# Differential attention: softmax difference, row sums and output squares moved off GpSimd and ScalarE onto VectorE

## The chip, the cores and the metric

The kernel runs on one core of one Trainium2 chip. The core has five engines with a queue each: TensorE (PE in the profile, with its weight loads as PEld), VectorE (DVE), ScalarE (ACT), GpSimd (POOL) and SyncE (SP), which here only issues DMAs. Each engine takes its instructions in the order in which they stand in its queue, and an instruction that waits holds up those behind it. The metric is the device time of one execution in microseconds (us).

## The reference

A two-layer encoder trunk for 1024 tokens of 1024 features, in float32. Layer 0 mixes tokens by differential attention, layer 1 by a state-space scan; each is followed by an MLP. The change touches layer 0's attention alone, cut here to its core:

```python
def block(q_blk):
    scores = jnp.einsum('bqhcd,bkhcd->bhcqk', q_blk, k, preferred_element_type=jnp.float32)
    p = jax.nn.softmax(scores, axis=-1)
    attn = (p[:, :, 0] - lam * p[:, :, 1]).astype(v.dtype)
    return jnp.einsum('bhqk,bkhe->bqhe', attn, v)

o = lax.map(block, qb)
o = o.transpose(1, 0, 2, 3, 4).reshape(b, s, N_HEADS, V_HEAD_DIM)
o = rms_norm(o, subln_gain) * (1.0 - lam_init)
return o.reshape(b, s, D_MODEL) @ w_o
```

There are 8 heads; each has two score maps (c = 0, 1) of 1024 x 1024, whose softmaxes are subtracted with the factor lambda before the product with the values. A head's output, 128 features per token, is then normalised by its root mean square.

## The kernel before

The program runs through the norm of x, the projections q, k and v, the attention, the output projection, the first MLP (beside which the state-space layer's matrices are prepared), the state-space layer with its gate, and the second MLP. Nearly all of it is bound to large matmuls.

The attention is cut into 64 tiles: 8 heads (h) times 8 blocks of 128 queries (qt). One tile passes through these steps, each a function of the kernel:

- `scores` (L395 to 407): for each of the two maps m, four matmuls of 512 columns into one `pss` of two banks: two against `kh`, the keys' high parts, and then two against `kl`, their low parts. There are two `pss`, so the scores of a tile's map wait until the exponentials of the same map in the tile before have read theirs.
- `maxima` (L409): one VectorE reduction of 128 x 1024 for each map.
- `exps` (L416): one ScalarE exponential for each map into `e0`, `e1`, with the row sums `s` written beside it.
- `combine` (L426): the factor `al` from the two row sums (a reciprocal and one more VectorE operation of one column), then `pd` = e0 + al * e1. It is done in two parts. Of the last 704 columns VectorE forms al * e1 (L434) and GpSimd adds e0 (L435); the first 320 columns VectorE does in one operation (L436). Then VectorE squares the row sum s0 into a column of `s2h` (L437).
- `transposes` (L440): eight transposes of `pd` on TensorE into two banks `pT`; `evacuate` (L450): ScalarE copies them to `pt`; `values` (L456): eight products with V into `po`. In the trace each of these eight float32 products is two records.
- `keep` (L462): ScalarE copies `po` to `osb` (L466), and then squares it with a sum into `ssh` (L467).

Once per head, `norm_o` adds `s2h` and `ssh`, takes the inverse root and scales `osb` (L476), and `turn_o` transposes it into `oT`, which ScalarE and VectorE (L485) split into high and low parts. `load_ops` (L382) loads a map's `q` (512 KB), `kh` and `kl` (two pieces of 256 KB each) from DRAM over SP's queue. There are three slots for each of the three, so the loads for a new head's second map wait until the scores of the first map of the last tile of the head before have been read from theirs.

The loops write the steps in a staggered order (`CF["order"]`), but a scheduler decides the order of the instructions in each engine's queue from its own estimates: another set of instructions can bring another order everywhere in the attention.

Of the kernel before, what the change touches and what calls it, by code (L numbers as in the profile page):

```python
# [10 lines left out]
F32 = mybir.dt.float32  # L11
# [6 lines left out]
P = 128  # L18
# [20 lines left out]
class WStream:  # L39
    """Weight tiles in the order of their use: loaded and split `ahead` tiles before that."""  # L40
# [50 lines left out]
def _build(ctx, tc, nc, a, out):  # L91
# [24 lines left out]
    # weights in the order of use  # L116
# [39 lines left out]
    # quarters of the columns by how much of their sums is done ahead: k 0 and 1, k 0 to 3, nothing  # L156
# [19 lines left out]
    def mm3(ps, w, n0, xs, nk=KT, halves=None):  # L176
        """ps [128, 1024] = W[:, n0:n0+128]^T X, in three passes that carry float32."""
# [13 lines left out]
    def mmh(ps, w, n0, xs, ks, t, start, stop):  # L191
        """The same for the k of one half and the tokens of one half."""
        c = slice(t * 512, t * 512 + 512)
        last = len(ks) - 1
        for kk, k in enumerate(ks):
            for i, (wt, x) in enumerate(((w[0], xs[0]), (w[0], xs[1]), (w[1], xs[0]))):
                nc.tensor.matmul(  # L197
                    ps, wt[:, kk, n0 : n0 + P], x[k][:, c], start=start and kk == 0 and i == 0, stop=stop and kk == last and i == 2
                )

    # ---------------------------------------------------------------- norm of x, transposed
# [5 lines left out]
    with tc.tile_pool(name="p0", bufs=8) as p0, tc.tile_pool(name="ps0", bufs=4, space=PSUM) as ps0:  # L207
# [46 lines left out]
        # lambda, on every partition  # L254
# [14 lines left out]
    # ---------------------------------------------------------------- q, k, v  # L269
# [100 lines left out]
    # ---------------------------------------------------------------- attention  # L370
# [7 lines left out]
    with tc.tile_pool(name="pb", bufs=2) as pb, tc.tile_pool(name="psb", bufs=2, space=PSUM) as psb:  # L378
# [13 lines left out]
        def scores(h, qt):  # L392
            if qt == 0:
# [3 lines left out]
                    small.tile([P, KT], F32, name="s2h", tag="s2h"),  # L397
# [18 lines left out]
        def exps(h, qt):  # L416
            w = work[h, qt]
            for m in range(2):
                e = pb.tile([P, S], F32, name=f"e{m}", tag=f"e{m}", bufs=CF["e"])
                s = small.tile([P, 1], F32, name="s", tag="s", bufs=6)  # L420
# [4 lines left out]
        def combine(h, qt):  # L425
            w = work[h, qt]  # L426
            s2h = heads[h][2]
            es, sums = w["e"], w["s"]
            al = small.tile([P, 1], F32, name="al", tag="al", bufs=4)
            nc.vector.reciprocal(al, sums[1])  # L430
            nc.vector.scalar_tensor_tensor(al, al, nlam, sums[0], op0=ALU.mult, op1=ALU.mult)
            pd = pb.tile([P, S], F32, name="pd", tag="pd", bufs=CF["pd"])
            n = CF["sp"]
            nc.vector.tensor_scalar(pd[:, n:], es[1][:, n:], al, None, op0=ALU.mult)  # L434
            nc.gpsimd.tensor_tensor(pd[:, n:], pd[:, n:], es[0][:, n:], op=ALU.add)  # L435
            nc.vector.scalar_tensor_tensor(pd[:, :n], es[1][:, :n], al, es[0][:, :n], op0=ALU.mult, op1=ALU.add)  # L436
            nc.vector.scalar_tensor_tensor(s2h[:, qt : qt + 1], sums[0], EPS * P, sums[0], op0=ALU.mult, op1=ALU.mult)  # L437
# [24 lines left out]
        def keep(h, qt):  # L462
            osb, ssh, s2h = heads[h]
# [3 lines left out]
            nc.scalar.activation(junk, osb[:, qt, :], AF.Square, accum_out=ssh[:, qt : qt + 1])  # L467

        def norm_o(h):
            osb, ssh, s2h = heads[h]  # L470
            # 1 / sqrt(mean o^2 + eps s0^2)
            rn = small.tile([P, KT], F32, name="rn", tag="rn")
            nc.vector.tensor_tensor(rn, s2h, ssh, op=ALU.add)
            nc.scalar.activation(rn, rn, AF.Ln, scale=1.0 / P)
# [17 lines left out]
        with tc.manual_schedule() if CF["man"] else ExitStack():  # L492
            stage = dict(S=scores, E=evacuate, K=keep, C=combine, M=maxima, X=exps, V=values, T=transposes)
            for i in range(n + 9):
# [8 lines left out]
                # a head's output, spread over the next tiles  # L503
# [11 lines left out]
    # ---------------------------------------------------------------- output projection, residual  # L515
# [7 lines left out]
    def acc_tile(name):  # L523
        """Two banks, as a tile or as two."""
# [7 lines left out]
    def pieces(ps):  # L532
        """(columns, bank or banks) of an accumulator."""
# [7 lines left out]
    class Norm:  # L541
        """The mean square of h over its features, as they come."""
# [26 lines left out]
        def per_token(self, rtok):  # L569
            """1 / root mean square as [c, j], token 8 c + j."""  # L570
# [52 lines left out]
    # ---------------------------------------------------------------- MLP  # L623
# [73 lines left out]
    # ---------------------------------------------------------------- S5 and GLU  # L697
# [83 lines left out]
class Prep:  # L781
    """The state-space layer's matrices, from its parameters alone, into DRAM.

    Rows of the state are (direction, p). Per group of channels:
    IN  [(j,h), (direction, re|im, p)]   a^(7-j) Bbar forward, a^j Bbar backward
    Y   [(direction, p), (re|im, j, h)]  Re and -Im of C a^(j+1) forward, C a^(8-j) backward
    K   [h', lag + 7, h]                 the kernel within a chunk of 8 tokens, with the skip
    R   [(direction, p), (cos|sin, n)]   of the angle of a^8 times n
    """
# [12 lines left out]
    def start(self, ps_pool, pool):  # L802
# [10 lines left out]
        # parameters as [(direction, p), g]  # L813
# [37 lines left out]
        # angles: theta, and 8 theta 2^k  # L851
# [22 lines left out]
        # (a - 1) / lambda  # L874
# [14 lines left out]
        # powers: a^l forward, a^(7-l) backward  # L889
# [16 lines left out]
        # mask of the diagonal blocks and of the diagonal  # L906
        self.mask = kp("mask", (P, 8))
        nc.gpsimd.memset(self.mask, 1.0)
        # keep where 0 <= p - 16 g <= 15
        nc.gpsimd.affine_select(self.mask, self.mask, [[-16, 8]], ALU.is_ge, 0.0, base=0, channel_multiplier=1)  # L910
        nc.gpsimd.affine_select(self.mask, self.mask, [[16, 8]], ALU.is_ge, 0.0, base=15, channel_multiplier=-1)
        # [p, h] = (p mod 16 == h)
# [7 lines left out]
        # skip times the norm's gain, by feature  # L920
# [6 lines left out]
    def tile(self, kt):  # L927
# [8 lines left out]
        def cmul(o, x, y, op, tmp, E=nc.gpsimd):  # L936
            """o = x[0] x[1] op y[0] y[1]"""
# [4 lines left out]
        # B, with the norm's gain  # L942
# [15 lines left out]
        # C and C a  # L958
# [17 lines left out]
        # the kernel at lag 0, both directions, and the skip  # L976
# [16 lines left out]
        # B by direction, zero in the other's rows  # L993
# [8 lines left out]
        for hf in range(4):  # L1002
# [8 lines left out]
            # IN, transposed  # L1011
# [14 lines left out]
            # Y  # L1026
# [4 lines left out]
            # the kernel at lags 1..8, [(lag, h), h']  # L1031
# [11 lines left out]
            # the rotation  # L1043
# [218 lines left out]
```

## Time and profile before

| | us |
|---|---|
| median of 3 runs | 2617.03 |
| lowest and highest run | 2615.14 and 2620.7 |
| span of the profiled execution | 2618.1 |
| of it, from the first scores to the first matmul of the output projection | 368.4 |

The profile is of one execution. The page gives each engine's busy time over the span, and the chain of work that ended last. A view by stretches gives each engine's busy time between two moments, with the granted clock of TensorE (1.00 is 2.4 GHz). A view of groups gives the mean length of equal instructions. A view in order of time gives the start of each instruction, its length and, in square brackets, how long its engine stood idle ahead of it and what ended that. Lengths of following instructions overlap a little, since engines are pipelined; what one costs in a full queue is read from start to start.

### The profile page before, as it was taken

The page shows a single profiled execution, that of the slowest core. Times are in us where ns is not written, and L with a number is a line of the kernel's source. Part 1 is how long each engine was busy: PE and PEld are TensorE (multiplying, and loading weights), DVE is VectorE, ACT ScalarE, POOL GpSimd, SP SyncE. Part 2 cuts the span into 40 slices and gives each one's busy share as a digit, 9 for nine tenths or more (in the row PEclk, how much of TensorE's full clock was granted, in tenths as well). Part 3 has the DMA queues.
Part 4 walks back from the last instruction along what each step waited for, and adds up shares of the span by engine and source line. Part 5 has one row for each costly group of instructions (what it writes and reads, how often), then busy time and mean ns, then how long its engine had stood idle before and what let it go on. Part 6 is the DMA issues. An engine that isn't in the chain of part 4 may idle for free.

```text
span 2618.1 us, 33770 instructions
## 1 busy us (share of the span) xinstructions
PE 2496.8 (95%) x12530; PEld 2071.0 (79%) x12530; DVE 1621.5 (62%) x3441; ACT 981.9 (38%) x1801; POOL 391.7 (15%) x452
## 2 busy tenths in 40 slices
PE   7999988888999999999999997899999999999998
PEld 6889877777777778788788876787888888888887
DVE  5664299999558987987973457994533333333332
ACT  5654276666433122122122137882331122112212
POOL 1211033333101431332341230000000000000000
PEclk9999999999999999999999998999999999999999
DMA  5768124131211222322332236553211111111112
GB/s 155 191 171 203 55 50 97 49 87 35 76 47 52 90 86 81 90 86 82 93 93 57 77 131 185 164 145 98 65 47 49 49 49 49 49 49 49 49 49 65
DMA packets 264964, 225.22 MB, mean 86 GB/s; under 512 B 41696, under 2 KB 248160, under 8 KB 264800
## 3 DMA queue, kind: packets, MB, share of 16 engines
q1 hardware_dynamic: 258912, 214.44, 28.8%
q10 hardware_dynamic: 5888, 8.63, 1.3%
q8 instruction: 99, 1.62, 0.3%
q14 instruction: 65, 0.53, 0.1%
HBM read 163.31 MB, written 51.31 MB: 82 GB/s over the span
## 4 chain that ended last, share of the span: by engine, by line
PE 61%; DVE 26%; ACT 4%; DMA 4%; issue 3%; SPq 1%; POOL 0%; DVEq 0%; ACTq 0%; POOLq 0%
PE psd L183 19%; PE psu L183 19%; PE psq L183 7%; DVE s2h L437 3%; DVE mx L413 3%; PE psw L183 3%; PE psh L197 3%; DVE tr L939 3%; DVE Rt L940 2%; ACT e L421 2%; DVE Rt L938 2%; DMA Rd<-Rt 2%; PE psg L183 2%; DVE wlo L67 2%; DVE pd L434 1%
## 5 line engine op out<-in xcount | busy, mean ns | idle before, releaser
L66 ACT ACTIVATE whi<-wraw 128x1024 fp32r<-128x1024 f32 (+1 forms) x177 | 186.8, 1055 | 971.1 <-PE psu L183 445.7
L658 DVE TENSOR_TENSOR hT<-hT,psd 128x1024 f32<-128x1024 f32 (+1 forms) x153 | 158.6, 1042 | 282.1 <-PE psd L183 282.1
L183 PE MATMUL psd<-sh,wlo 128*128 128x512 f32 x1024 | 332.3, 400 | 0.0
L183 PE MATMUL psd<-sh,whi 128*128 128x512 f32 x1024 | 328.0, 399 | 1.7 <-ACT ob L612 1.7
L183 PE MATMUL psd<-sl,whi 128*128 128x512 f32 x1024 | 326.7, 398 | 0.0
L183 PE MATMUL psu<-ah_u,whi 128*128 128x512 f32 x1024 | 318.7, 392 | 0.0
L183 PE MATMUL psu<-ah_u,wlo 128*128 128x512 f32 x1024 | 316.9, 391 | 0.0
L183 PE MATMUL psu<-al_u,whi 128*128 128x512 f32 x1024 | 316.8, 391 | 0.0
L67 DVE TENSOR_TENSOR wlo<-wraw,whi 128x1024 fp32r<-128x1024 f32 (+1 forms) x177 | 219.2, 1239 | 95.5 <-ACT whi L66 95.2
L640 DVE SCALAR_TENSOR_TENSOR mz<-psu,nacc 128x512 f32<-128x512 f32 x128 | 82.9, 685 | 281.5 <-PE psu L183 272.5
L183 PEld LDWEIGHTS psd<-sl,whi 128*128 128x128 f32 x1024 | 190.9, 188 | 44.4
L183 PEld LDWEIGHTS psd<-sh,whi 128*128 128x128 f32 x1024 | 190.0, 188 | 45.5 <-ACT ob L612 3.1
L183 PEld LDWEIGHTS psd<-sh,wlo 128*128 128x128 f32 x1024 | 191.1, 188 | 43.5
L183 PEld LDWEIGHTS psu<-ah_u,whi 128*128 128x128 f32 x1024 | 192.0, 188 | 42.1 <-issue 1.7
L183 PEld LDWEIGHTS psu<-al_u,whi 128*128 128x128 f32 x1024 | 192.4, 188 | 39.9
L183 PEld LDWEIGHTS psu<-ah_u,wlo 128*128 128x128 f32 x1024 | 192.1, 188 | 39.9
L421 ACT ACTIVATE e<-pss,mx 128x1024 f32<-128x1024 f32 x128 | 142.7, 1115 | 117.0 <-DVE mx L413 116.1
L435 POOL TENSOR_TENSOR pd<-pd,e 128x704 f32<-128x704 f32 x64 | 117.9, 1842 | 342.2 <-DVE pd L434 131.0
L413 DVE TENSOR_REDUCE mx<-pss 128x1 f32<-128x1024 f32 x128 | 150.8, 1210 | 2.4 <-PE pss L406 2.3
L460 PE MATMUL po<-V,pt 128*128 128x128 f32 x1024 | 136.1, 276 | 0.7 <-ACT pt L454 0.7
L460 PEld LDWEIGHTS po<-V,pt 128*128 128x128 f32 x1024 | 130.5, 193 | 6.8 <-ACT pt L454 1.1
L406 PE MATMUL pss<-kh,q 128*128 128x512 f32 x256 | 92.8, 444 | 42.0 <-ACT e L421 37.5
(311 smaller groups left out, 4361.3 us busy)
## 6 DMA issues: line engine op xcount, KB each, us to landing
wraw<-in_ffn_w_up_dram SPq DMA_DIRECT2D x64, 512.0 KB, 4.0
wraw<-in_ffn_w_down_dram SPq DMA_DIRECT2D x64, 512.0 KB, 3.5
wraw<-in_attn_w_qkv_dram SPq DMA_DIRECT2D x24, 512.0 KB, 6.1
xt<-in_x_dram SPq DMA_DIRECT2D x16, 512.0 KB, 6.4
zs<-z ACTq DMA_DIRECT2D x64, 128.0 KB, 5.2
q<-qs SPq DMA_DIRECT2D x16, 512.0 KB, 6.6
kh<-ks SPq DMA_DIRECT2D x32, 256.0 KB, 6.9
kl<-ks SPq DMA_DIRECT2D x32, 256.0 KB, 7.7
```

The costliest lines, as they stand in the source:

```text
L66: self.nc.scalar.activation(hi, t, AF.Copy)
L67: self.nc.vector.tensor_tensor(lo, t, f32(hi), op=ALU.subtract)
L183: nc.tensor.matmul(ps[t] if isinstance(ps, list) else ps[:, c], wt[:, k, n0 : n0 + P], x[k][:, c], start=k == 0 and i == 0, stop=k == nk - ...
L197: nc.tensor.matmul(ps, wt[:, kk, n0 : n0 + P], x[k][:, c], start=start and kk == 0 and i == 0, stop=stop and kk == last and i == 2)
L406: nc.tensor.matmul(ps[:, c], q[:, qt * P : (qt + 1) * P], k[:, c], start=i == 0, stop=i == 1)
L413: nc.vector.tensor_reduce(mx, w["ps"][m], axis=AX.X, op=ALU.min)
L421: nc.scalar.activation(e, w["ps"][m], AF.Exp, bias=w["mx"][m], scale=-1.0, accum_out=s)
L435: nc.gpsimd.tensor_tensor(pd[:, n:], pd[:, n:], es[0][:, n:], op=ALU.add)
L437: nc.vector.scalar_tensor_tensor(s2h[:, qt : qt + 1], sums[0], EPS * P, sums[0], op0=ALU.mult, op1=ALU.mult)
L460: nc.tensor.matmul(w["po"], w["pt"][:, k, :], V[:, k, h * P : (h + 1) * P], start=k == 0, stop=k == KT - 1)
L640: nc.vector.scalar_tensor_tensor(z, bank(ps, t), 0.0, rbc[:, c], op0=ALU.max, op1=ALU.mult)
L658: nc.vector.tensor_tensor(hT[:, m, c], hT[:, m, c], p, op=ALU.add)
```

## The change

In `combine` the three operations that form `pd` become one VectorE operation over all 1024 columns (L433 of the new kernel), and GpSimd has no part in the attention any more. The 64 squares of a row sum (L437) go: the exponentials now write their row sums into columns of a tile `sums` that is kept for a head, and `norm_o` squares them once per head (L471). In `keep` the square and sum of `osb` move from ScalarE to VectorE, in one operation that multiplies `po`, still in PSUM, by `osb` and writes the sum beside it (L463). `al` is formed by another form of operation of one column (L431). The factor 1/P moves from one place of the norm to another. The rest of the diff strips comments.

```diff
-                    small.tile([P, KT], F32, name="s2h", tag="s2h"),
+                    small.tile([P, 2, KT], F32, name="sums", tag="sums"),
...
-                s = small.tile([P, 1], F32, name="s", tag="s", bufs=6)
+                s = heads[h][2][:, m, qt : qt + 1]
                 nc.scalar.activation(e, w["ps"][m], AF.Exp, bias=w["mx"][m], scale=-1.0, accum_out=s)
...
             nc.vector.reciprocal(al, sums[1])
-            nc.vector.scalar_tensor_tensor(al, al, nlam, sums[0], op0=ALU.mult, op1=ALU.mult)
+            nc.vector.tensor_scalar(al, al, nlam, sums[0], op0=ALU.mult, op1=ALU.mult)
             pd = pb.tile([P, S], F32, name="pd", tag="pd", bufs=CF["pd"])
-            n = CF["sp"]
-            nc.vector.tensor_scalar(pd[:, n:], es[1][:, n:], al, None, op0=ALU.mult)
-            nc.gpsimd.tensor_tensor(pd[:, n:], pd[:, n:], es[0][:, n:], op=ALU.add)
-            nc.vector.scalar_tensor_tensor(pd[:, :n], es[1][:, :n], al, es[0][:, :n], op0=ALU.mult, op1=ALU.add)
-            nc.vector.scalar_tensor_tensor(s2h[:, qt : qt + 1], sums[0], EPS * P, sums[0], op0=ALU.mult, op1=ALU.mult)
+            nc.vector.scalar_tensor_tensor(pd, es[1], al, es[0], op0=ALU.mult, op1=ALU.add)
...
             nc.scalar.activation(osb[:, qt, :], w["po"], AF.Copy)
-            nc.scalar.activation(junk, osb[:, qt, :], AF.Square, accum_out=ssh[:, qt : qt + 1])
+            nc.vector.scalar_tensor_tensor(
+                junk, w["po"], 1.0 / P, osb[:, qt, :], op0=ALU.mult, op1=ALU.mult, accum_out=ssh[:, qt : qt + 1]
+            )
...
+            s2 = small.tile([P, KT], F32, name="s2", tag="s2")
+            nc.vector.scalar_tensor_tensor(s2, sums[:, 0, :], EPS, sums[:, 0, :], op0=ALU.mult, op1=ALU.mult)
             rn = small.tile([P, KT], F32, name="rn", tag="rn")
-            nc.vector.tensor_tensor(rn, s2h, ssh, op=ALU.add)
-            nc.scalar.activation(rn, rn, AF.Ln, scale=1.0 / P)
+            nc.vector.tensor_tensor(rn, s2, ssh, op=ALU.add)
+            nc.scalar.activation(rn, rn, AF.Ln)
```

The scheduler gives the attention another order on TensorE, VectorE and ScalarE; from the output projection on, the order is the one of before. Two places matter below.

VectorE in the middle of a head, before: one tile from one pair of maxima (`mx`, one for each map) to the next.

```order
L413 TENSOR_REDUCE mx<-pss 128x1 x2
L430 RECIPROCAL al<-s 128x1
L431 SCALAR_TENSOR_TENSOR al<-al,nlam,s 128x1
L434 TENSOR_SCALAR pd<-e_3620,al 128x704
L436 SCALAR_TENSOR_TENSOR pd<-e_3620,al,e_3617 128x320
L437 SCALAR_TENSOR_TENSOR s2h<-s 128x1
L413 TENSOR_REDUCE mx<-pss 128x1 x2
```

VectorE in the middle of a head, in the changed kernel:

```order
L430 RECIPROCAL al<-sums 128x1
L431 TENSOR_SCALAR al<-al,nlam,sums 128x1
L433 SCALAR_TENSOR_TENSOR pd<-e_3546,al,e_3544 128x1024
L413 TENSOR_REDUCE mx<-pss 128x1
L463 SCALAR_TENSOR_TENSOR junkb,ssh<-po,osb 128x128
L413 TENSOR_REDUCE mx<-pss 128x1
L430 RECIPROCAL al<-sums 128x1
```

The square of the row sum no longer stands ahead of the maxima, and the new sum of squares (of a tile two or more back) stands between the two maxima, so that one of them is behind a wait for ScalarE's copy of `po`.

TensorE at the start of the third head (tile 16), before: from the scores of its first map (the first two rows) to those of its second (the last two).

```order
L406 MATMUL pss<-kh,q 128x512 x2
L406 MATMUL pss<-kl,q 128x512 x2
L460 MATMUL po<-V,pt 128x128 x4
L447 MATMUL pT<-ident,pd 128x128 x2
L460 MATMUL po<-V,pt 128x128 x4
L447 MATMUL pT<-ident,pd 128x128 x6
L406 MATMUL pss<-kh,q 128x512 x2
L406 MATMUL pss<-kl,q 128x512 x2
```

TensorE at the same place in the changed kernel:

```order
L406 MATMUL pss<-kh,q 128x512 x2
L406 MATMUL pss<-kl,q 128x512 x2
L443 MATMUL pT<-ident,pd 128x128 x8
L406 MATMUL pss<-kh,q 128x512 x2
L406 MATMUL pss<-kl,q 128x512 x2
L456 MATMUL po<-V,pt 128x128 x8
```

The products with V have moved behind the scores of the second map, so these stand closer to those of the first. At other heads' starts four of the eight products stay ahead of them.

## Rows read from the trace of the kernel before

**Rows 1.** The page: busy time of each engine; shares of the chain that ended last.

```profile
PE 2496.8 (95%) x12530; PEld 2071.0 (79%) x12530; DVE 1621.5 (62%) x3441; ACT 981.9 (38%) x1801; POOL 391.7 (15%) x452
...
PE 61%; DVE 26%; ACT 4%; DMA 4%; issue 3%; SPq 1%; POOL 0%; DVEq 0%; ACTq 0%; POOLq 0%
```

**Rows 2.** By stretches, the attention: from:to, length, PE, PEld, DVE, ACT, POOL, PEclk, DMA.

```profile
312.24:680.62 368.38, 322.82 (x2067) 268.18 (x2065) 349.39 (x474) 250.90 (x594) 116.03 (x63) 0.99 0.24 59
```

**Rows 3.** Groups in the attention: count, busy us, mean ns of one, idle before.

```profile
L421 ACT ACTIVATE e<-pss,mx 128x1024 f32<-128x1024 f32 x128 | 142.7, 1115 | 117.0 <-DVE mx L413 116.1 <-DVE al L430 0.6 <-issue 0.3
...
L437 DVE SCALAR_TENSOR_TENSOR s2h<-s 128x1 f32<-128x1 f32 x64 | 101.7, 1589 | 0.2 <-ACT e L421 0.2
...
L436 DVE SCALAR_TENSOR_TENSOR pd<-e,al,e 128x320 f32<-128x320 f32 x63 | 34.4, 546 | 0.0
...
L467 ACT ACTIVATION_READ_ACCUMULATOR junkb<-osb 128x1 f32 x61 | 13.3, 218 | 0.0
L485 DVE SCALAR_TENSOR_TENSOR al_o<-oT,gsub,ah_o 128x512 fp32r<-128x512 f32 x14 | 10.3, 735 | 0.0
...
L476 DVE TENSOR_TENSOR osb<-osb,rn 128x1024 f32<-128x1024 f32 x7 | 8.5, 1212 | 0.0
```

**Rows 4.** In order of time, one tile: start, length, engine, line, operation [idle before].

```profile
490.07 0.59 DVE L434 TENSOR_SCALAR pd<-e,al 128x704 f32<-128x704 f32 x1
...
490.57 0.55 DVE L436 SCALAR_TENSOR_TENSOR pd<-e,al,e 128x320 f32<-128x320 f32 x1
...
490.76 0.73 PE L406 MATMUL pss<-kh,q 128*128 128x512 f32 x2
...
490.83 1.84 POOL L435 TENSOR_TENSOR pd<-pd,e 128x704 f32<-128x704 f32 x1 [3.70 <-PE pss L406]
...
491.04 1.65 DVE L437 SCALAR_TENSOR_TENSOR s2h<-s 128x1 f32<-128x1 f32 x1
...
491.79 1.05 PE L460 MATMUL po<-V,pt 128*128 128x128 f32 x8
...
492.61 2.34 DVE L413 TENSOR_REDUCE mx<-pss 128x1 f32<-128x1024 f32 x2
492.68 0.38 PE L447 MATMUL pT<-ident,pd 128*128 128x128 f32 x2
...
493.79 0.82 PE L447 MATMUL pT<-ident,pd 128*128 128x128 f32 x6
...
495.09 0.17 DVE L430 RECIPROCAL al<-s 128x1 f32<-128x1 f32 x1
...
495.11 0.73 PE L406 MATMUL pss<-kh,q 128*128 128x512 f32 x2 [0.50 <-ACT e L421]
...
496.30 0.73 PE L406 MATMUL pss<-kh,q 128*128 128x512 f32 x2
```

**Rows 5.** In order of time, the fourth tile of the first head.

```profile
335.34 0.15 DVE L437 SCALAR_TENSOR_TENSOR s2h<-s 128x1 f32<-128x1 f32 x1
...
335.49 1.69 POOL L435 TENSOR_TENSOR pd<-pd,e 128x704 f32<-128x704 f32 x1 [4.07 <-DVE s2h L437]
```

**Rows 6.** In order of time: last tile of the fourth head, its load's first and last issue.

```profile
484.78 0.73 PE L406 MATMUL pss<-kh,q 128*128 128x512 f32 x2
...
485.55 0.44 SPq L388 DMA_DIRECT2D kh<-ks  x1
...
487.80 0.59 SPq L389 DMA_DIRECT2D kl<-ks  x1
```

**Rows 7.** Instructions on `kl`, issues from 391 to 394.5, then from 485 to 488.5.

```profile
DMA to landing us min/median/max: 8.6/9.2/9.8
...
DMA to landing us min/median/max: 4.9/5.6/6.3
```

**Rows 8.** In order of time and by stretches (columns as in rows 2): the third head's start.

```profile
403.50 1.22 PE L406 MATMUL pss<-kl,q 128*128 128x512 f32 x2 [0.43 <-DMA kl<-ks]
...
403.50:406.30 2.80, 2.80 (x7) 2.22 (x8) 1.81 (x2) 0.31 (x2) 0.56 (x1) 0.50 0.73 138
```

More of the change, by code (lines that the diff above doesn't have):

```diff
@@ L426, in combine @@
             w = work[h, qt]
-            s2h = heads[h][2]
             es, sums = w["e"], w["s"]
@@ L462, in keep @@
         def keep(h, qt):
-            osb, ssh, s2h = heads[h]
+            osb, ssh, _ = heads[h]
             w = work.pop((h, qt))
@@ L466, in keep @@
             nc.scalar.activation(osb[:, qt, :], w["po"], AF.Copy)
-            nc.scalar.activation(junk, osb[:, qt, :], AF.Square, accum_out=ssh[:, qt : qt + 1])
+            nc.vector.scalar_tensor_tensor(
+                junk, w["po"], 1.0 / P, osb[:, qt, :], op0=ALU.mult, op1=ALU.mult, accum_out=ssh[:, qt : qt + 1]
+            )
         def norm_o(h):
-            osb, ssh, s2h = heads[h]
+            osb, ssh, sums = heads[h]
+            s2 = small.tile([P, KT], F32, name="s2", tag="s2")
+            nc.vector.scalar_tensor_tensor(s2, sums[:, 0, :], EPS, sums[:, 0, :], op0=ALU.mult, op1=ALU.mult)
             rn = small.tile([P, KT], F32, name="rn", tag="rn")
-            nc.vector.tensor_tensor(rn, s2h, ssh, op=ALU.add)
-            nc.scalar.activation(rn, rn, AF.Ln, scale=1.0 / P)
+            nc.vector.tensor_tensor(rn, s2, ssh, op=ALU.add)
+            nc.scalar.activation(rn, rn, AF.Ln)
             nc.scalar.activation(rn, rn, AF.Exp, scale=-0.5)
```

## Prediction

> **What bounds the kernel now.** I read the page first: TensorE is busy 95% of the span and holds 61% of the chain that ended last, but VectorE holds 26% of it [rows 1]. So there is a stretch where VectorE decides, and the change lies in one. By stretches, from the first scores to the first matmul of the output projection, 368.4 us, VectorE is busy 349.4 (95%), TensorE 322.8 (88%), ScalarE 250.9 and GpSimd 116.0 [rows 2]. This stage is bound to VectorE, TensorE not far behind; outside it the queues keep their order, so the forecast is what these 368.4 us become.
>
> One tile in order of time shows why [rows 4]. TensorE starts a tile's scores at 490.76 and the same step of the next at 496.30: a tile takes 5.54 us. VectorE's part from start to start: product over 704 columns 0.50, fused operation over 320 columns 0.47, square of a row sum 1.57, and 3.00 for the rest (two maxima, reciprocal, factor). In those 3.00 it waits once, from the end of the maxima at 494.95 to the reciprocal at 495.09, 0.14. TensorE waits for an exponential (0.50 are marked), and that is late because its maximum is.
>
> The square is the odd row. It touches one column and lasts 1589 ns in the mean of 64 [rows 3]. It starts at 491.04, just after GpSimd's addition at 490.83, and ends at 492.69, where that ends, at 492.67 [rows 4]. Where it came ahead of GpSimd it took 0.15 [rows 5]. So it is not work: a VectorE operation with two inputs in SBUF stands still while GpSimd's runs, and both maxima are queued behind it.
>
> **The change part by part.** *Removed from VectorE, a tile:* 0.50 + 0.47 + 1.57 = 2.54 us [rows 4]. I drop the 0.14 wait too, since other work now stands between the second exponential and the reciprocal that needs its sum; if it stays, it costs 9 us in all. What is left is 2.86.
>
> *Added, the difference in one operation:* 1024 columns. The fused operation over 320 takes 546 ns, an operation with two SBUF inputs over 1024 takes 1212 [rows 3]: (1212 - 546) / 704 = 0.95 ns a column above 0.24 fixed, so 1.2 us. It lies on VectorE's path, and waits for no other engine.
>
> By the Trainium skill's Vector Engine (DVE) Microarchitecture Reference, section Points that are easy to get wrong, a `scalar_tensor_tensor` with two non-bf16 SBUF sources runs at half throughput. By that rule the new operation would take about 2.2 us and the sum would turn round; it is a rival below. The trace disagrees: the 320 columns, both sources float32 in SBUF, took 546 ns with everything [rows 3].
>
> *Added, the sum of squares:* 128 columns with one input in PSUM. Nearest is the operation over 512 columns out of PSUM, 735 ns [rows 3]; 384 columns less at 0.95 make 0.37. No VectorE operation of before writes a sum beside its output. ScalarE's read of such a sum takes 0.22 [rows 3], so the bounds are 0.37 and 0.59, and I take 0.45. It waits for ScalarE's copy of the output, and the next maximum is queued behind it. The copy is of a tile two or more back and its product is long done, so I take the wait at nothing; uncovered, it costs the exponential that may stand ahead of the copy, 1.1 [rows 3].
>
> *VectorE's new sum:* 2.86 + 1.2 + 0.45 = 4.51 a tile. Per head come the scaling (1.21), two splits (0.735 each) [rows 3] and two small operations of 0.15 each (as the free square [rows 5]): 3.0. A head is 8 x 4.51 + 3.0 = 39.1.
>
> *TensorE's sum,* unchanged in work, from start to start [rows 4]: four score matmuls 1.03 (490.76 to 491.79), eight records of the product with V 0.89, two transposes 0.22 (of the 1.11 from 492.68 to 493.79). A tile has 2 x 1.03 + 2 x 0.89 + 0.88 = 4.72, a head 8 x 4.72 and eight more transposes, 38.6. The two engines become equal: TensorE is the next bound right behind. Walking the new order through a head's end with these lengths, I find TensorE waiting for a few tenths at most.
>
> *ScalarE* loses the square (off the path); *GpSimd* is empty. `al` in another form costs the same.
>
> *The stage without transfers:* 8 x 39.1 = 313, and 7 (an estimate, one and a half tiles) to fill and empty the pipeline: 320.
>
> *The loads.* SP's queue issues the same loads at the same events; but tiles get shorter and transfers do not. The loads for a head's second map are released by the first scores of the last tile before. These start at 484.78, the first issue follows at 485.55 (0.77) and the last, of `kl`, at 487.80 (2.25 on) [rows 6]. The last piece lands 9.8 us after its issue in the third head and 6.3 in the fifth [rows 7]; three of the seven head starts are like the first, four like the second. So the data are there 12.8 or 9.3 us after those scores. Before, the second map's scores came at 495.11 [rows 4], 10.3 after them, and only the slow loads made TensorE wait [rows 8]. Now the second map's scores come after one tile (4.72) and what stands between the two maps: 1.03 + 0.88 in the order shown for the third head, 0.89 more where four products stay ahead. With half a group for the `kh` part they need `kl` after 7.1 to 8.0, say 7.6. The waits are 3 x 5.2 + 4 x 1.7 = 22. After such a wait the granted clock was 0.50, 1.2 GHz, for the 2.8 us from 403.50 [rows 8], where half the work got done: 1.4 lost, 4 for the three long waits. Together 26.
>
> *Sum:* 320 + 26 = 346 against 368.4, 22 less. The span was 2618.1, 1.1 above the median of 2617.0; taken from the median this is **2595**.
>
> **The rivals.**
> *The loads do not hurt.* If all land as in the fifth head or sooner and the waits fall where VectorE is behind anyway, the stage is 320 and the time 2569. For it: VectorE's extra work per head falls in the tiles right behind the wait. Against: the slow landings were there in three heads of seven.
> *The engines trade waits.* With two engines of equal load and two score buffers, an order made by estimates can cost each tile some tenths. At 0.2 a tile 13 us more, less 3 because the loads then have more time: 2605. For it: the order differs from head to head. Against: before, TensorE's waits all lead back to VectorE.
> *The long operation runs at half rate.* At 1.89 ns a column it takes 2.2, a VectorE tile 5.5, a head 46.9 against 368.4 / 8 = 46.05 before, so 7 us slower, 2624. Against it is the 546 ns row, where 320 columns at that rate would need 605 without the fixed part.
> *The sum of squares waits, the other side.* If ScalarE's copy stands behind an exponential that itself waits for a maximum, the VectorE operation costs 0.45 + 1.1 = 1.55 with the next maximum behind it. A head is then 8 x 5.61 + 3.0 = 47.9, 15 us more over eight heads, 2632. It is slower from a cost of 1.3 on. Against: the copy belongs to a tile long past.
> *The change does not do what it says:* the stall is not tied to GpSimd, and another VectorE operation inherits it. Then 1.4 a tile comes back, a head is 8 x 5.91 + 3.0 = 50.3, 34 us more than now in all, 2651. The 0.15 us square [rows 5] speaks against it.
>
> **How the numbers follow.** Forecast 0.60; loads hidden 0.14; traded waits 0.17; half rate 0.02; waiting sum 0.04; inherited stall 0.01; 0.02 for what I do not see. The low end reaches to the case without load waits, 2570; the high end takes in the traded waits and the sum of squares at 0.59, 2610. No change that can be measured means within 0.2%, some 5 us, about what the runs differ by. Traded waits at twice my price would land there: faster 0.87, same 0.06, slower 0.07.
>
> **What would show it.** In the changed kernel's trace: no VectorE row of one column above 0.25 us; the difference at 1.2 us; the sum of squares at 0.4 to 0.6 with its read; tiles of 4.6 to 4.8 us in mid-head, with TensorE hardly waiting; at each head's start a TensorE wait ended by the `kl` or `kh` transfer, 4 to 6 us in the first three, 1 to 2 later, and a granted clock of 0.5 behind the long ones; the stage some 346 us. The forecast is wrong if the difference takes 2 us, if mid-head tiles stay above 5 us, or if the head starts show no wait.

## The result and the profile after

The changed kernel takes 2572.2 us (median of four runs, 2566.6 to 2574.7), the kernel before in the same session 2618.4 (2615.1 to 2620.7). The ratio is 0.982 with a 95% interval of 0.9806 to 0.9835. The gain is 46 us where 22 were forecast: the sign and the mechanism came out, the size is more than double. The time lies in the range, near its low end.

The profiled executions differ by 46.7 us (spans 2618.1 and 2571.4), and three stretches share them. The attention, from the first scores to the first matmul of the output projection, went from 368.4 to 328.45 us: 39.9. What lies ahead of it is 1.1 shorter (it starts at 311.14 instead of 312.24), what lies behind it 5.7 (1931.8 instead of 1937.5).

The page of the changed kernel, busy time of each engine and shares of the chain that ended last; the answer to [rows 1]:

```profile
PE 2483.1 (97%) x12530; PEld 2077.8 (81%) x12530; DVE 1557.6 (61%) x3449; ACT 965.3 (38%) x1673; POOL 272.3 (11%) x388
...
PE 73%; DVE 17%; DMA 4%; ACT 3%; issue 3%; SPq 1%; POOL 0%; ACTq 0%; DVEq 0%; POOLq 0%
```

By stretches, the attention of the changed kernel (from:to, length, PE, PEld, DVE, ACT, POOL, granted clock, DMA share, GB/s); the answer to [rows 2]:

```profile
311.14:639.59 328.45, 311.44 (x2075) 274.35 (x2073) 283.83 (x477) 235.72 (x474) 0.00 (x0) 0.97 0.27 67
```

VectorE's share of the chain fell from 26% to 17%, and in the attention it is busy 283.8 of 328.45 us (86%), where it was 349.4 of 368.4. TensorE is now busy 95% of the stage: the bound has changed hands.

Groups in the attention of the changed kernel (count, busy us, mean ns of one, idle before); these answer to [rows 3]:

```profile
L413 DVE TENSOR_REDUCE mx<-pss 128x1 f32<-128x1024 f32 x128 | 155.7, 1221 | 22.6 <-PE pss L406 21.7
...
L433 DVE SCALAR_TENSOR_TENSOR pd<-e,al,e 128x1024 f32<-128x1024 f32 x64 | 82.0, 1282 | 1.2
...
L463 DVE SCALAR_TENSOR_TENSOR junkb<-po,osb 128x128 f32<-128x128 f32 x63 | 17.8, 283 | 12.6 <-ACT osb L462 12.6
...
L463 DVE DVE_READ_ACCUMULATOR junkb<-po,osb 128x1 f32 x63 | 5.3, 84 | 0.0
...
L471 DVE SCALAR_TENSOR_TENSOR s<-sums 128x8 f32<-128x8 f32 x8 | 1.3, 159 | 0.0
```

The 64 squares of 1589 ns are gone; what squares the row sums now is eight operations of 159 ns. The fused difference is the one long new row, 1282 ns. The sum of squares costs 283 ns and a read of its sum 84. The maxima, VectorE's largest group, now wait for TensorE's scores (21.7 us).

One tile in the middle of a head of the changed kernel, in order of time (start, length, engine, line, operation [idle before]); the answer to [rows 4]:

```profile
481.35 0.71 PE L406 MATMUL pss<-kh,q 128*128 128x512 f32 x2
...
482.36 0.60 PE L443 MATMUL pT<-ident,pd 128*128 128x128 f32 x4
...
482.56 1.23 DVE L413 TENSOR_REDUCE mx<-pss 128x1 f32<-128x1024 f32 x1 [0.59 <-PE pss L406]
...
482.80 1.06 PE L456 MATMUL po<-V,pt 128*128 128x128 f32 x8
...
483.69 0.60 PE L443 MATMUL pT<-ident,pd 128*128 128x128 f32 x4
483.70 0.15 DVE L430 RECIPROCAL al<-sums 128x1 f32<-128x1 f32 x1
...
483.89 0.27 DVE L431 TENSOR_SCALAR al<-al,nlam,sums 128x1 f32<-128x1 f32 x1
...
484.05 0.71 PE L406 MATMUL pss<-kh,q 128*128 128x512 f32 x2
...
484.20 1.28 DVE L433 SCALAR_TENSOR_TENSOR pd<-e,al,e 128x1024 f32<-128x1024 f32 x1
...
485.05 1.05 PE L456 MATMUL po<-V,pt 128*128 128x128 f32 x8
...
485.40 0.29 DVE L463 SCALAR_TENSOR_TENSOR junkb<-po,osb 128x128 f32<-128x128 f32 x1
...
485.61 0.09 DVE L463 DVE_READ_ACCUMULATOR junkb<-po,osb 128x1 f32 x1
...
485.61 1.22 DVE L413 TENSOR_REDUCE mx<-pss 128x1 f32<-128x1024 f32 x1
...
485.86 0.48 PE L406 MATMUL pss<-kh,q 128*128 128x512 f32 x1
```

TensorE takes 4.51 us from its scores at 481.35 to the same step at 485.86, and none of its rows is marked with a wait. VectorE's chain from the reciprocal at 483.70 to the end of the sum at 485.61 is 1.91; with two maxima of 1.23 and 1.22 that is 4.36 or less, and the maximum at 482.56 stood idle for 0.59 ahead of it, for TensorE.

The start of the third head in the changed kernel, TensorE and SP in order of time and then by stretches; these answer to [rows 6] and [rows 8]:

```profile
385.00 0.70 PE L406 MATMUL pss<-kh,q 128*128 128x512 f32 x2
...
393.02 0.70 PE L406 MATMUL pss<-kh,q 128*128 128x512 f32 x2 [1.22 <-DMA kh<-ks]
394.09 0.73 PE L406 MATMUL pss<-kl,q 128*128 128x512 f32 x2 [0.37 <-DMA kl<-ks]
```

```profile
385.73 0.44 SPq L388 DMA_DIRECT2D kh<-ks  x1
...
387.99 0.59 SPq L389 DMA_DIRECT2D kl<-ks  x1
```

```profile
391.00:394.09 3.09, 1.51 (x11) 0.86 (x9) 2.82 (x4) 2.64 (x6) 0.00 (x0) 1.00 1.04 247
394.09:398.00 3.91, 3.91 (x19) 3.82 (x20) 1.23 (x1) 0.00 (x0) 0.00 (x0) 0.59 1.04 254
```

The loads are released by the last tile's first scores at 385.00; the last piece of `kl` is issued at 387.99 and lands at 394.09, 6.1 us later. TensorE waits 1.6 us for the two tiles, and for the next 3.9 us its granted clock is 0.59 in the mean, between its two levels of 2.4 and 1.2 GHz: most of this stretch ran at 1.2 GHz.

```profile
394.80:398.20 3.40, 3.40 (x18) 3.40 (x17) 1.23 (x1) 0.04 (x1) 0.00 (x0) 0.50 1.09 230
```

TensorE's waits in the attention of the changed kernel, with what ended them (us in total, times, longest); 1.5 us more are waits for ScalarE's copies:

```profile
PE pss L406 <- DMA kh<-ks: 5.1, 5, 1.9
PE pss L406 <- ACT e L421: 4.0, 7, 2.0
PE pss L406 <- issue: 3.4, 2, 1.8
PE pss L406 <- DMA kl<-ks: 2.7, 6, 0.5
...
```

The same view of the kernel before, whose rows were not shown:

```profile
PE pss L406 <- ACT e L421: 37.5, 52, 2.0
...
PE pss L406 <- DMA kl<-ks: 1.8, 3, 0.8
PE pss L406 <- DMA kh<-ks: 1.4, 1, 1.4
...
```

Before, the exponentials took 37.5 us of TensorE's waits and the loads 3.2. Now the exponentials take 4.0 and the loads 7.8.

### The profile page after: what moved, and what is told of

Read it like the earlier page. It is cut to its first block, busy times and chain, and to the rows that moved or that the text cites. A ratio compares the mean times of both kernels' runs of the same rounds, so it can differ in the third digit from the quotient of the medians.

```text
span 2571.4 us, 33566 instructions
## 1 busy us (share of the span) xinstructions
PE 2483.1 (97%) x12530; PEld 2077.8 (81%) x12530; DVE 1557.6 (61%) x3449; ACT 965.3 (38%) x1673; POOL 272.3 (11%) x388
## 4 chain that ended last, share of the span: by engine, by line
PE 73%; DVE 17%; DMA 4%; ACT 3%; issue 3%; SPq 1%; POOL 0%; ACTq 0%; DVEq 0%; POOLq 0%
PE psu L183 22%; PE psd L183 21%; PE psq L183 7%; PE pss L406 4%; PE psw L183 3%; PE po L456 3%; PE psh L197 3%; DVE tr L939 2%; DVE Rt L940 2%; PE psg L183 2%; DMA kl<-ks 2%; DVE Rt L938 1%; DVE wlo L67 1%; PE pT L443 1%; DVE s L1156 1%
## 5 line engine op out<-in xcount | busy, mean ns | idle before, releaser
L183 PEld LDWEIGHTS psd<-sh,whi 128*128 128x128 f32 x1024 | 190.1, 188 | 45.1 <-ACT ob L612 3.1
L183 PEld LDWEIGHTS psu<-al_u,whi 128*128 128x128 f32 x1024 | 192.4, 188 | 39.9
L413 DVE TENSOR_REDUCE mx<-pss 128x1 f32<-128x1024 f32 x128 | 155.7, 1221 | 22.6 <-PE pss L406 21.7
L940 DVE TENSOR_TENSOR Rt<-Rt,tr 128x2 f32<-128x2 f32 (+6 forms) x448 | 102.5, 229 | 6.3
```

Of the source, the lines that this page charges most:

```text
L183: nc.tensor.matmul(ps[t] if isinstance(ps, list) else ps[:, c], wt[:, k, n0 : n0 + P], x[k][:, c], start=k == 0 and i == 0, stop=k == nk - ...
L413: nc.vector.tensor_reduce(mx, w["ps"][m], axis=AX.X, op=ALU.min)
L940: E.tensor_tensor(o, o, tmp, op=op)
```

## The experiments

The theory: GpSimd's addition holds VectorE up, ending that makes the two engines nearly equal, and the loads at the heads' starts then cost time. The main rivals: the gain is VectorE's shorter work and not the stall; the loads cost nothing. Twelve runs were made in three groups, each beside the kernel before on the same chip (medians 2619.5, 2618.5 and 2618.9). "Stage" is the attention as above, from each kernel's profiled execution.

The traces also show which edits brought another order. In the attention, e4 and e7 have the changed kernel's order of instructions on TensorE, VectorE and ScalarE, e8 that of the kernel before, e9 that of e6 and e10 that of e5. So the loads and the fourth slot are tried in an unchanged order. Runs e2, e3, e5 and e6 each have an order of their own, and their times contain it.

| run | median us (lowest to highest) | ratio, 95% interval | stage us | behind it us |
|---|---|---|---|---|
| e1 changed again | 2571.7 (2566.8 to 2574.0) | 0.981 (0.979 to 0.983) | 327.5 | 1933.1 |
| e2 sums only | 2574.8 (2573.9 to 2577.9) | 0.982 (0.980 to 0.984) | 325.9 | 1938.7 |
| e3 fused only | 2580.4 (2576.9 to 2582.6) | 0.984 (0.982 to 0.986) | 335.5 | 1932.3 |
| e4 no loads | 2550.7 (2549.3 to 2553.7) | 0.973 (0.971 to 0.975) | 308.6 | 1928.2 |
| e5 sum on ScalarE | 2579.7 (2572.3 to 2584.3) | 0.985 (0.983 to 0.987) | 333.1 | 1927.2 |
| e6 sum twice | 2563.4 (2561.1 to 2564.8) | 0.979 (0.978 to 0.981) | 320.7 | 1929.0 |
| e7 four kl | 2554.8 (2551.5 to 2557.5) | 0.976 (0.974 to 0.977) | 311.6 | 1932.3 |
| e8 before, no loads | 2614.7 (2612.3 to 2616.6) | 0.9985 (0.9975 to 0.9994) | 367.6 | 1933.6 |
| e9 twice, no loads | 2551.7 (2550.0 to 2553.8) | 0.975 (0.973 to 0.976) | 308.3 | 1930.9 |
| e10 ScalarE, no loads | 2560.3 (2559.1 to 2561.7) | 0.978 (0.976 to 0.979) | 315.2 | 1933.8 |
| e11 before again | 2619.2 (one run) | | 368.4 | 1937.1 |
| e12 changed third | 2573.5 (one run) | | 328.3 | 1932.3 |

### The same kernels again

Runs e1 and e12 are the changed kernel, e11 is the kernel before, all with no edit.

> The changed kernel once more, beside the experiments on the same chip. Two parts of its gain are to be told apart: the attention (from its first scores to the first matmul of the output projection) went from 368.4 to 328.5 us, and what follows it from 1937.5 to 1931.8, although its queues kept their order. If the 5.7 us behind the attention are chance from one execution to the next, this run's trace shows another value there, anywhere from 1931 to 1938. If they belong to the change, it shows 1931 to 1933 again. The whole: 2567 to 2575 us.

> The kernel before once more, for a second profile of what follows the attention: 1937.5 us in the first one, 1931.8 and 1933.1 in two of the changed kernel. If this length is chance, it falls between 1927 and 1939 again, below 1935 as well as not. If the change shortens it, it is 1936 to 1939.

> The changed kernel a third time, for the same question: 1927 to 1939 behind the attention if it is chance, 1931 to 1934 if it belongs to the change. The attention 327 to 329.

The stage repeats to 1.0 us over three executions of the changed kernel (327.5 to 328.5), and to 0.1 over two of the kernel before. What lies behind it repeats too: 1931.8, 1933.1 and 1932.3 against 1937.5 and 1937.1. So the 5 us there are not the chance of one execution.

### One half of the change at a time

In e2 the split between VectorE and GpSimd stays, and ScalarE's square of the output; the row sum's square leaves `combine`, and `norm_o` does it once per head. `al` takes its new form too.

```diff
-                s = small.tile([P, 1], F32, name="s", tag="s", bufs=6)
+                s = heads[h][2][:, m, qt : qt + 1]
...
-            nc.vector.scalar_tensor_tensor(al, al, nlam, sums[0], op0=ALU.mult, op1=ALU.mult)
+            nc.vector.tensor_scalar(al, al, nlam, sums[0], op0=ALU.mult, op1=ALU.mult)
...
-            nc.vector.scalar_tensor_tensor(s2h[:, qt : qt + 1], sums[0], EPS * P, sums[0], op0=ALU.mult, op1=ALU.mult)
...
+            nc.vector.scalar_tensor_tensor(s2h, sums[:, 0, :], EPS * P, sums[:, 0, :], op0=ALU.mult, op1=ALU.mult)
```

> Of the change only the square of the row sum is taken out of the tile (row sums kept per head, squared once); GpSimd still adds 704 columns and ScalarE still squares the output. Theory (the stall was all): VectorE's tile falls from 5.54 by 1.57 to some 4.0 us, TensorE's 4.5 us is the bound, no other VectorE operation meets GpSimd's, and the time is that of the changed kernel, 2565 to 2580. Rival (the fused difference is what gains, or the stall passes to the next operation with two SBUF inputs): 2595 or more.

Groups in the attention of e2; the columns are as above:

```profile
L434 POOL TENSOR_TENSOR pd<-pd,e 128x704 f32<-128x704 f32 x64 | 117.9, 1842 | 299.7 <-DVE pd L433 168.8 <-ACT osb L464 47.5 <-ACT e L421 24.0
...
L476 DVE TENSOR_TENSOR osb<-osb,rn 128x1024 f32<-128x1024 f32 x7 | 13.0, 1861 | 0.0
...
L470 DVE SCALAR_TENSOR_TENSOR s<-sums 128x8 f32<-128x8 f32 x8 | 7.6, 948 | 0.0
...
L473 DVE TENSOR_TENSOR rn<-s,ssh 128x8 f32<-128x8 f32 x7 | 4.3, 618 | 0.0
```

GpSimd adds as long as before, 1842 ns, and the stage is 325.9 us all the same, as short as with the whole change. It follows that GpSimd's work by itself was not the cost; the VectorE operation queued behind its start was. The stall has not vanished either: the three operations of `norm_o` with two inputs in SBUF inherit it. The new square of eight columns takes 948 ns where it takes 159 without GpSimd, the scaling 1861 where it took 1212 [rows 3]. But they come once per head and not once per tile.

In e3 only the difference is fused; the 64 squares and ScalarE's sum stay.

```diff
-            n = CF["sp"]
-            nc.vector.tensor_scalar(pd[:, n:], es[1][:, n:], al, None, op0=ALU.mult)
-            nc.gpsimd.tensor_tensor(pd[:, n:], pd[:, n:], es[0][:, n:], op=ALU.add)
-            nc.vector.scalar_tensor_tensor(pd[:, :n], es[1][:, :n], al, es[0][:, :n], op0=ALU.mult, op1=ALU.add)
+            nc.vector.scalar_tensor_tensor(pd, es[1], al, es[0], op0=ALU.mult, op1=ALU.add)
```

> Of the change only the difference in one VectorE operation, without GpSimd; the square of the row sum stays in each tile, ScalarE still squares the output. Theory (the stall was all): the square takes 0.15 us again, VectorE's tile is some 4.3 us, under TensorE's 4.5, and the time is that of the changed kernel, 2565 to 2580. Rival (a square per tile costs by itself): 1.4 us a tile stay, over 2600.

Groups in the attention of e3:

```profile
L433 DVE SCALAR_TENSOR_TENSOR pd<-e,al,e 128x1024 f32<-128x1024 f32 x64 | 82.2, 1285 | 2.3
...
L434 DVE SCALAR_TENSOR_TENSOR s2h<-s 128x1 f32<-128x1 f32 x64 | 9.6, 150 | 0.2 <-ACT e L421 0.2
```

The same 64 squares take 150 ns instead of 1589, with the same inputs. GpSimd is idle now; their place in VectorE's queue is another one too, but in the kernel before the square that came ahead of GpSimd's addition also took 0.15 us [rows 5]. That is the stall, shown by the row itself. The two halves alone bring 33 (e3) and 42 us (e2) of the stage, where both together bring 40: they remove the same wait, one by taking away what waited and the other by taking away what was waited for, and whichever comes second has only TensorE's bound left to gain from. Part of the difference between them is the loads: the profile marks 12.1 us of TensorE's waits with `kh` and `kl` in e3 and 5.2 in e2. At 2580.4 us e3 lies at the upper edge of what the theory gave it.

### What the loads cost

In e4 every head computes with the first head's `q`, `kh` and `kl`, so the loads of the other seven heads are left out; e8 does the same to the kernel before. Both compute something other than attention.

```diff
-                            load_ops(h + 1, 0 if qt == CF["l0"] else 1)
+                            m = 0 if qt == CF["l0"] else 1
+                            ops[2 * (h + 1) + m] = ops[m]
```

> The changed kernel without the loads of the heads' operands after the first head: every head computes with the first head's q and k, so that part of the computation is left out. It measures what the loads cost. The forecast's step: 26 us, so some 2546. Theory now, by the tiles at the heads' starts of the changed kernel's trace: some 20 us (16 of waits, 3 to 4 of the lower clock behind them), 2549 to 2556, the attention 309. Rival (the waits fall where VectorE would be late anyway): under 8 us, 2564 or more.

> The kernel before without the loads after the first head (every head computes with the first head's q and k; that part is left out). It tells whether the shorter tiles uncovered the loads or whether they cost as much before. Theory (they were hidden under VectorE's longer tiles but for the third and fourth head): 1 to 6 us faster than before, 2612 to 2617. Rival: 15 us or more, under 2603.

By stretches, the attention of e4 (columns as above):

```profile
310.36:618.96 308.60, 302.04 (x2075) 269.48 (x2073) 283.56 (x477) 234.71 (x474) 0.00 (x0) 0.99 0.02 4
```

All of TensorE's waits in the attention of e8, from 311.70 us to 679.29:

```profile
PE pss L406 <- ACT e L421: 40.1, 61, 2.1
PE po L460 <- ACT pt L454: 0.7, 1, 0.7
```

Without loads the changed kernel gains 20.9 us (2571.7 to 2550.7; stage 19.9), and the kernel before 3.9, of which its stage shows 0.8. Before, the loads hid behind waits for the exponential that came anyway: without them TensorE waits 40.1 us for exponentials where it waited 37.5, and hardly for anything else. The change uncovered the loads.

Against the changed kernel e4 splits the 19.9 us in two: TensorE's matmuls, the same 2075 records, are busy 302.0 us instead of 311.4, which makes 9.4; and TensorE is idle for the rest of the stage, 6.6 us instead of 17.0, which makes 10.4. Of the 9.4 the granted clock accounts for 6.8. It was 0.50 behind the waits at four heads' starts (from 353.9, 394.8, 439.2 and 599.6 us), 13.6 us in all, of which half is lost; e4 has no such stretch there. What the other 2.6 us are is not shown. The split also differs between executions of the same kernel. The attention of e1 and of e12, by stretches:

```profile
311.52:638.98 327.46, 308.02 (x2075) 271.07 (x2073) 283.77 (x477) 235.53 (x474) 0.00 (x0) 0.98 0.27 67
311.14:639.39 328.25, 309.58 (x2074) 272.29 (x2073) 283.73 (x477) 235.70 (x474) 0.00 (x0) 0.97 0.27 67
```

Against e4 these are 6.0 and 7.5 us longer busy and 12.9 and 12.1 longer idle; their clock fell at two heads and at three. So the waits cost more than the lower clock behind them, which takes 3 to 7 of the 19 to 20 us.

In e7 `kl` has four slots instead of three, so its loads no longer wait for the last tile of the head before. Everything is computed.

```diff
-            kl = pb.tile([P, S], F32R, name="kl", tag="kl", bufs=CF["op"])
+            kl = pb.tile([P, S], F32R, name="kl", tag="kl", bufs=CF["op"] + 1)
```

> The changed kernel with a fourth slot for the keys' low parts, so that a third of a new head's second load (0.5 of 1.5 MB) no longer waits for the last tile of the head before. Theory (the waits are the time of the transfer): about a third of the load's time is saved at each of seven heads' starts, 2 us each, 8 to 16 us, 2556 to 2564. Rival (the wait is latency, not volume): 0 to 4 us, 2568 or more.

By stretches, the attention of e7, and its waits of TensorE for loads, from 312 us to 615:

```profile
311.27:622.86 311.59, 302.57 (x2074) 269.10 (x2073) 283.80 (x477) 234.91 (x474) 0.00 (x0) 0.99 0.27 68
```

```profile
PE pss L406 <- DMA kh<-ks: 2.5, 2, 1.3
```

One more slot of 4 KB per partition gives back 17 of the 20 us, at the same bytes and the same DMA share, and more than the 8 to 16 that the theory gave it. `kl` no longer appears among the waits, `kh` twice instead of five times, and the two unexplained "issue" waits (3.4 us) are gone, which speaks for counting them to the loads. At 2554.8 us this kernel is faster than both: 63.8 below the kernel before of its group, 17 below the changed one.

### The sum of squares: where it stands and what it costs

In e5 the sum of the output's squares goes back to ScalarE; in e6 VectorE does it twice, the second time for nothing. Runs e9 and e10 are e6 and e5 without the loads, cut as in e4.

```diff
# e5
-            nc.vector.scalar_tensor_tensor(
-                junk, w["po"], 1.0 / P, osb[:, qt, :], op0=ALU.mult, op1=ALU.mult, accum_out=ssh[:, qt : qt + 1]
-            )
+            nc.scalar.activation(junk, osb[:, qt, :], AF.Square, scale=P ** -0.5, accum_out=ssh[:, qt : qt + 1])
# e6
+            nc.vector.scalar_tensor_tensor(
+                junk, w["po"], 1.0 / P, osb[:, qt, :], op0=ALU.mult, op1=ALU.mult, accum_out=ssh[:, qt : qt + 1]
+            )
```

> The changed kernel with one part undone: ScalarE squares and sums the output again. VectorE's tile falls by some 0.25 us, ScalarE's rises by some 0.5. Theory (TensorE's 4.5 us a tile is the bound): no difference, 2567 to 2577. Rival (VectorE decides, the forecast's 39.1 us a head): 64 x 0.25 = 16 us faster, 2557 or less.

> The changed kernel with the sum of squares on VectorE done twice in each tile: it prices this operation and VectorE's slack. Theory (VectorE's tile is 4.25 us, TensorE's 4.5): the second one, some 0.3 us, mostly fills slack, 0 to 8 us, 2570 to 2582. Rival (VectorE decides): 64 x 0.3 = 19 us and more, 2590 or more.

> The changed kernel with the sum of squares done twice and without the loads after the first head (every head computes with the first head's q and k; that part is left out). With the loads, doing it twice was 8 us faster than the changed kernel, which more work alone can't bring. Theory (the scheduler's other order sets the new head's second scores some 1.6 us further from the scores that release their load, so less of the load is waited for): without loads the advantage is gone, 0 to 8 us slower than the changed kernel without loads, 2550 to 2559, the attention 308 to 316. Rival (the other order is better for the engines themselves): again 8 us faster, 2544 or less, the attention 301.

> The sum of squares on ScalarE, without the loads after the first head (every head computes with the first head's q and k; that part is left out). Theory (TensorE is the bound of a tile, and the 5 us by which the attention of this version was longer came of the loads and the other order): the attention is 305 to 312 as without loads in the changed kernel, 2547 to 2555. Rival (VectorE decides): 10 us and more below it, 2540 or less.

With one more VectorE operation in every tile e6 is faster than the changed kernel by 8 us, and without loads the advantage is gone (2551.7 against 2550.7; stages 308.3 and 308.6). VectorE is busy 293.9 us of the stage in e9 instead of 283.6 in e4, and the stage takes as long. So in this order the operation costs nothing, VectorE is not the bound, and what e6 gained hung on the loads. The theory for e6 (no faster than 2570) was wrong. The order of its TensorE queue gives a reason. TensorE at the start of its third head, from the last tile's scores before it:

```profile
386.33 0.72 PE L406 MATMUL pss<-kh,q 128*128 128x512 f32 x2 [0.65 <-ACT e L421]
...
389.94 0.70 PE L406 MATMUL pss<-kh,q 128*128 128x512 f32 x2
...
390.95 0.63 PE L406 MATMUL pss<-kh,q 128*128 128x512 f32 x2
...
391.87 1.05 PE L456 MATMUL po<-V,pt 128*128 128x128 f32 x8
392.76 0.60 PE L443 MATMUL pT<-ident,pd 128*128 128x128 f32 x4
393.20 1.06 PE L456 MATMUL po<-V,pt 128*128 128x128 f32 x8
394.09 0.60 PE L443 MATMUL pT<-ident,pd 128*128 128x128 f32 x4
394.99 0.70 PE L406 MATMUL pss<-kh,q 128*128 128x512 f32 x2 [0.30 <-DMA kh<-ks]
```

Between the first map's scores of the new head (390.95) and the second's (394.99) stand eight products (sixteen records) and eight transposes, where the changed kernel has the transposes alone. From the scores that release the loads (386.33) to these it is 8.4 us without the wait of 0.30; in the changed kernel, from 385.00 to 393.02 without its 1.22, it is 6.8. So the loads have 1.6 us more. That the order is the cause is an inference: no run changed it alone.

Taking the sum off VectorE again makes it slower, with loads (e5, by 8 us) and without (e10, by 9.6; stage 315.2 against 308.6). The theory had expected no loss, with loads or without, and missed both times; a VectorE that is the bound would have made e10 faster, so that rival fell too. Heads in the middle of e10 take 39.1 us each; in e4 they take 37.3 and 39.4 in turn. Whether ScalarE's added operation or the order that comes with it does this, no run tells apart.

## Why the prediction was right and wrong

**The mechanism was right.** The square was a wait for GpSimd and no work: e3's 150 ns shows it, and e2 shows that removing the waiting operation is enough. The loads came out from under the exponentials as predicted (e4 against e8), the granted clock fell behind them, and the bound moved to TensorE. *Inherited stall* fell with rows of 159 ns and less; *half rate* fell with 1282 ns for 1024 columns; the *waiting sum of squares* costs 12.6 us of idle VectorE, in a stage in which VectorE has time. *Loads do not hurt* fell with e4. *Traded waits* fell too: TensorE waits 4.0 us for exponentials in the whole stage.

**Luck.** The time lies in the forecast's range, but 3 us from the price of a rival that fell (*the loads do not hurt*, 2569). The loads did cost 19.9 us; a stage 11 us shorter than forecast and 6.8 us outside it hid that in the total.

**Right sizes.** The fused difference: forecast 1.2, measured 1.20 from start to start (484.20 to 485.40). A short load wait: forecast 1.7; at the third head 1.6, with the data there 9.1 us after the releasing scores (forecast 9.3), though for this head the long wait of 5.2 had been forecast. `al` in its new form is longer, 272 ns in the mean instead of 220, above the 0.25 us named as a sign of a stall, but from start to start it takes 0.31 (483.89 to 484.20), no more than the 0.33 of before.

**The step that failed first: the stage without transfers, 320 against 308.6 in e4.** Two terms were too large. The sum of squares, taken at 0.45 within bounds of 0.37 and 0.59, takes 0.21 from start to start (485.40 to 485.61): the lower bound was scaled from an instruction's whole length, the upper one added a read's whole length to it, and in a full queue both overlap what follows. With it VectorE's tile is at most 4.36 instead of 4.51. By these sums alone the engines stay close (a head of VectorE 8 x 4.36 + 3.0 = 37.9 at most); that VectorE no longer sets the time is shown by e9, and by TensorE being busy 302.0 of e4's 308.6 us. TensorE's tile was put at 4.72 (and tiles of 4.6 to 4.8 named as what would show it) and is 4.51: four scores take 1.00 to 1.01 instead of 1.03, eight products followed by scores 0.81 instead of 0.89 (485.05 to 485.86), four transposes followed by scores 0.36 instead of 0.44 (483.69 to 484.05). In front of each other, products and transposes take 0.89 and 0.44 here too (482.80 to 483.69, 482.36 to 482.80). What a step costs depends on what stands behind it, and before, the step ahead of the scores ended in a wait and could not be read. Over 64 tiles 0.21 is 13 us.

A head of TensorE is then 8 x 4.51 + 0.88 = 36.96, eight of them 295.7. With e4's 6.6 of waits 6.3 us of the 308.6 are left. They do not confirm the 7 us to fill and empty: they are time in which TensorE was busy. Some 3 of them come from a granted clock of 0.50 from 315.7 to 322.5 us, at the stage's start, with 6.07 us of TensorE busy, and heads in the middle take 37.3 and 39.4 in turn.

**The second: the loads, 26 against 19.9.** The long landing of 9.8 us, forecast for three heads, was there in none (in the kernel before itself the three were at most 8.8, 9.8 and 7.8): at the seven heads the last piece of `kl` landed 6.1 to 7.2 us after its issue. Instructions on `kl` in the changed kernel, issues from 345 us to 347 (the longest) and from 387 to 389 (the shortest), which answer to [rows 7]:

```profile
DMA to landing us min/median/max: 6.0/6.6/7.2
```

```profile
DMA to landing us min/median/max: 4.9/5.5/6.1
```

The waits for loads are thus 7.8 us, or 11.2 with the two that the profile calls "issue", instead of 22. On the other side the clock cost 6.8 instead of 4: it fell at four heads instead of three, one of them behind a wait of only 1.6 us, and cost 1.7 each time. The 1.4 of the forecast was read from a stretch cut off at 406.30; the granted clock was 0.50 until 406.9. Errors in opposite directions left 6 us. Why three of the landings of before took longer was not tried.

**The third: outside the stage, nothing forecast, 6.8 us measured.** Part of it repeats (about 5 us behind the attention). Its queues are nearly those of before: TensorE's matmuls of the output projection come in another order for the first 43 us, and from there on its order is the same. Nearly every edit of the attention moves this part, and either way: 1927.2 in e5, 1938.7 in e2, where the order of the first MLP is another too. But it also moves with the order kept: without the loads it is 3.6 us shorter in the changed kernel (e4) and 3.9 in the kernel before (e8). Where the 5 us arise does not repeat. Between the first two traces the same TensorE instructions are 41.2 us apart around 750 and 46.0 around 1280, in the first MLP; between e11 and the same trace of the changed kernel they are 45.1 apart around 750 already, and 46.1 at the end. No run looked into it, and its cause stays open. It limits what the medians tell: e2's whole median is 2.6 us above the changed kernel's, though its stage is 2.5 shorter.

**The sum put right:** 308.6 + 19.9 = 328.5, 40 us less than before, and 6.8 beside it: 46.7.

One slip changes nothing above: the prices of *half rate*, the *waiting sum of squares* and the *inherited stall* set a head without the 7 us to fill and empty against 368.4 / 8, which contains that time. Each should have been 7 us higher.

## What to carry to other kernels

The one-column operation that lasted over a microsecond was a wait in disguise. In such a case look for what runs on the neighbouring engine at the same moment, and try moving the small operation before the large one. When a stage becomes faster, the transfers that were hidden in its waits can come out, and one more buffer for the tile that lands last (4 KB per partition here) can be worth more than a third of what the change itself brought. Read the cost of a step from start to start in a stretch where its engine never waits, and with the step behind it that it will have; whole lengths put end to end, and distances read in front of another step, priced the tiles of both engines too high here.

## What the runs showed of the hardware that was not expected

- VectorE's read of a sum beside an operation takes 84 ns and costs nothing visible behind it, where ScalarE's takes 218 [rows 3]; operation and read together cost 0.21 us from start to start.
- The fused operation with two float32 sources in SBUF takes 1282 ns for 1024 columns and 546 for 320 [rows 3], 1.05 ns a column between the two. The rule of the Trainium skill's Vector Engine (DVE) Microarchitecture Reference, section Points that are easy to get wrong, that such an operation runs at half throughput, does not show at this size either.
- A wait of 1.6 us at a head's start was followed by a granted clock of 0.50 (from 394.8 to 398.2 us), which cost as much again, 1.7 us. Over the stage, in three executions of the changed kernel, such stretches cost 3 to 7 us and the waits 10 to 13.
- More work was faster: a useless VectorE operation in every tile made the kernel 8 us shorter, and without the loads that difference was gone.
